# Decoder trunk on one core: another order of loads, sums and transposes in the opening

## The chip, the cores and the metric

The kernel runs on one core of one Trainium2 chip. The metric is the device time of one execution in microseconds (us), lower is better. One profiled execution supplies every duration that is read from a trace.

## What is computed

The reference is a trunk of two decoder layers on one sequence of 256 positions and width 2048, in float32. The first layer mixes tokens by forgetting attention with 16 heads, the second by sliding-window attention with sinks. Each is followed by a gated feed-forward layer of width 5632 with a causal convolution of width 3. Every sub-layer is shifted, scaled and gated by vectors that come from one conditioning vector `c`.

```python
c_act = jax.nn.silu(c)
for i in range(DEPTH):                                   # DEPTH = 2
    mod = c_act @ ada_w[i] + ada_b[i]                    # (1, 2048) @ (2048, 12288)
    sh1, sc1, g1, sh2, sc2, g2 = jnp.split(mod[:, None, :], 6, axis=-1)
    h = x * (1.0 + sc1) + sh1
    y = fox_attention(h, ...) if i % 2 == 0 else swa_attention(h, ...)
    x = layer_norm(ALPHA * x + (1.0 + g1) * y, ln_mix_g[i], ln_mix_b[i])
    h = x * (1.0 + sc2) + sh2
    y = conv_ffn(h, ffn_w_up[i], ffn_conv_w[i], ffn_conv_b[i], ffn_w_down[i])
    x = layer_norm(ALPHA * x + (1.0 + g2) * y, ln_ffn_g[i], ln_ffn_b[i])
```

The change lies in the very first of these lines: shift and scale of layer 0 (`sh1`, `sc1`), the modulated input `h`, and the first products `h @ w_in` of the forgetting attention. What is computed stays the same.

## The kernel before, in words

Almost every product is made in three parts: the float32 weight tile `w` (256 rows by 512 columns, 512 KB) is loaded by the SyncE queue, ScalarE casts it to its high part `wh` (line 276), VectorE subtracts to get the low part `wl` (line 287), and TensorE multiplies high by high, high by low and low by high. The modulated input stands as a high and a low part too (`hHL`). One weight tile with its matmuls is called a product below. Ten tile buffers of 512 KB (the pool `wp`) hold all weights in flight, whatever their use; four `wh` and four `wl` buffers stand behind them.

Attention can start only when `h` is there, and `h` needs shift and scale, which are themselves a product of a vector with 2048 rows of `ada_w`. The function `opening` does this in eight steps. Step `cb` deals with one chunk of 256 columns of shift and 256 of scale: sixteen loads `wo` of 128 rows by 512 columns (256 KB each, two to a tile buffer, line 532), each multiplied by its element of `cact` and added to an accumulator `oacc` of 128 by 512. That is done by `sums`: GpSimd writes the accumulator by the first multiply (line 542), VectorE adds the other fifteen in order (line 547; one of them, row block 10 of step 0, is summed by TensorE instead, line 539). At the end of a step comes what is called a turn below: TensorE sums the accumulator over the partitions with four matmuls of one column against `ones` (tile `cps`, line 572; as float32 each is recorded as two passes), transposes two blocks of `x` (`mod_turn`, line 469, tile `sm`), VectorE adds the bias (`cv`, line 578) and `mod_pair` makes the high and low parts of `h` for these 256 columns (lines 478 to 482 in step 0, 484 to 486 and 85 to 86 later).

Beside the sums, steps 1 to 8 run products of the forgetting attention that need only chunks which are already turned. The table `plan` (line 860) names two items for each of the steps 1 to 7 and one for step 8; an item is three products (q, k, v), so six products fall on a step. Where an item's block of outputs is left for another, ScalarE copies its partial sums out of PSUM (line 886, tiles `part` and `spare`). `warm` (line 494) issues matmuls whose result nobody reads, to keep TensorE busy before real work. `x` is loaded 512 columns at a time, ahead of the even steps (line 567). `rotary` (lines 170 to 205) prepares tables for the second layer; its first two VectorE instructions (lines 176 and 178) wait for two small loads.

The program fixes the order of an engine's instructions where `pin` is used; elsewhere a list scheduler decides it when the program is built. The engines then run their own queues in order. After the opening the kernel goes on with products of the same kind to its end.

Of the kernel before, what the change touches and what calls it, by code (L numbers as in the profile page):

```python
# [17 lines left out]
P = 128  # L18
# [23 lines left out]
def hybrid_trunk(ctx: ExitStack, tc: tile.TileContext, a: dict, out: bass.AP):  # L42
# [127 lines left out]
    def rotary():  # L170
# [5 lines left out]
        nc.vector.tensor_scalar_mul(nsink, sink, -1.0)  # L176
        posf = cst.tile([NT, P], F32, name="posf")
        nc.vector.tensor_copy(posf, posr)
# [341 lines left out]
    def opening(plan, proj, also):  # L520
# [5 lines left out]

        def sums(cb, acc, ps):
            for kq in range(0, KC, QK):
                w = wp.tile([P, QK, 2, CB], F32, tag="w", name="wo")
                for k in range(QK):  # L530
                    kc = kq + k
                    nc.sync.dma_start(w[:, k], a["ada_w"][0, kc * P:(kc + 1) * P, :2 * D]
                                      .rearrange("p (v d) -> p v d", v=2)[:, :, cb * CB:(cb + 1) * CB])
                for k in range(QK):
                    kc = kq + k
                    wk = w[:, k].rearrange("p v f -> p (v f)")
                    if cb == 0 and kc == 10:
                        for c in range(4):
                            pin(mm(ps[:, c:c + 1], wk[:, c * P:(c + 1) * P], cact[:, kc:kc + 1], start=c == 0, skip_group_check=True))
                        warm(6)  # L540
                    elif kc == 0:
                        nc.gpsimd.tensor_scalar_mul(acc, wk, cact[:, kc:kc + 1])  # L542
                    elif cb == 1 and kc == 1:
                        with tc.issue_after(first_cv[0].ins):
                            nc.vector.scalar_tensor_tensor(acc, wk, cact[:, kc:kc + 1], acc, op0=ALU.mult, op1=ALU.add)
                    else:
                        nc.vector.scalar_tensor_tensor(acc, wk, cact[:, kc:kc + 1], acc, op0=ALU.mult, op1=ALU.add)  # L547
                yield

        first_cv = []  # L550
        accs = cst.tile([P, D], F32, tag="acc", name="oacc").rearrange("p (c a) -> p c a", a=2 * CB)
        for cb, items in enumerate(plan):
            k = 2 * cb
            todo = [(*it, part) for it in items for part in range(3)]
            n = len(todo)
            if cb == D // CB:
                for it in todo:
                    proj(*it)
                break
            acc = accs[:, cb % 4]  # L560
            ps = bank("cps")
            also.get(cb, lambda: None)()
            steps = [sums(cb, acc, ps)] * (KC // QK)
            for i, g in enumerate(steps):
                if i == 0 and cb % 2 == 0:
                    c = slice(cb * CB, (cb + 2) * CB)
                    nc.sync.dma_start(x[:, :, c], a["x"][0][:, c].rearrange("(t p) d -> p t d", p=P))
                next(g)
                while todo and n - len(todo) < (i + 1) * n // len(steps):
                    proj(*todo.pop(0))  # L570
            for c in range(4):
                pin(mm(ps[:, c:c + 1], acc[:, c * P:(c + 1) * P], ones[:, 0:1], start=cb > 0 and c == 0, stop=True,
                       skip_group_check=True), cb == 0)
            if cb == 0:
                warm(8)
            tps = mod_turn(k, 2 if cb == 0 else 1)
            for v in range(2):
                first_cv[:] = [nc.vector.scalar_tensor_tensor(cols[0, v][:, k:k + 2], ps[:, 2 * v:2 * v + 2], float(v),
                                                              acol[:, 0, v * KC + k:v * KC + k + 2],
                                                              op0=ALU.add, op1=ALU.add)]  # L580
            mod_pair(cols[0, 1], cols[0, 0], k, tps, cb == 0)
# [569 lines left out]
```

## Time and profile before

| | us |
|---|---|
| median of 3 runs (2270.6 to 2272.76) | 2271.17 |
| the profiled execution | 2271.15 |
| its span, first to last instruction | 2269.4 |
| TensorE busy / weight loads busy | 2202.8 / 1889.6 |
| VectorE busy | 1863.2 |
| ScalarE busy | 1184.0 |
| GpSimd busy | 35.7 |
| first product of the attention starts at | 30.76 |

How to read it: the profiled execution's own time is 1.75 us above its span and 0.02 us below the median, so a microsecond of its span counts as a microsecond of the median. Times in the rows are counted from the span's start. A row of the timeline gives start, duration, engine, line, operation, output and inputs, shape and count; in brackets stands how long the engine had been idle before it, and what ended that wait. Rows of several instructions are merged.

### The profile page before, as it was taken

The numbers are of one execution on the slowest core, as the hardware profiler recorded it, in microseconds if no ns is written. First come the engines' busy times: TensorE is split into PE (matmuls) and PEld (weight loads), VectorE is DVE, ScalarE is ACT, GpSimd is POOL, SyncE is SP. The second block draws the span as 40 slices with busy tenths as digits, with TensorE's granted clock in tenths as the row PEclk, the third lists the DMA queues.
The fourth block names the chain that finished last, engine by engine and source line by source line (L and its number), as shares of the span: only waits on it lengthen the run. The fifth ranks groups of instructions, "written<-read, shape, count | busy, mean of one in ns | idle before, by whom it ended". The sixth has DMA issues, their size and how long they took to land. (4 is left out here: it accounts for less than half of the span.)

```text
span 2269.4 us, 33231 instructions
## 1 busy us (share of the span) xinstructions
PE 2202.8 (97%) x12135; PEld 1889.6 (83%) x12135; DVE 1863.2 (82%) x2692; ACT 1184.0 (52%) x1859; POOL 35.7 (2%) x59
## 2 busy tenths in 40 slices
PE   5899999999999999999999999999999999999997
PEld 5789898788888888888887788888888888888886
DVE  6898998979988978878988989889988655666766
ACT  2435644455555533555534588746555533555642
POOL 1110000000000000000000000000000000000000
PEclk9999999999999999999999999999999999999999
DMA  9999999968977889878887876668887556666553
GB/s 333 346 336 323 346 354 356 323 233 293 327 254 249 300 315 324 284 241 280 283 299 278 271 239 225 232 252 288 285 275 243 185 193 191 190 189 194 187 195 111
DMA packets 287012, 602.67 MB, mean 266 GB/s; under 512 B 21814, under 2 KB 54776, under 8 KB 286336
## 3 DMA queue, kind: packets, MB, share of 16 engines
q1 hardware_dynamic: 285792, 595.86, 77.5%
q0 software_dynamic: 1056, 4.69, 0.6%
q8 instruction: 95, 1.56, 0.3%
q14 instruction: 69, 0.57, 0.1%
HBM read 598.37 MB, written 2.10 MB: 265 GB/s over the span
## 5 line engine op out<-in xcount | busy, mean ns | idle before, releaser
L276 ACT CAST wh<-w 128x1024 fp32r<-128x1024 f32 x728 | 763.5, 1051 | 789.0 <-PE wd L76 284.1
L287 DVE TENSOR_TENSOR wl<-w,wh 128x1024 fp32r<-128x1024 f32 x728 | 887.0, 1221 | 296.2 <-ACT wh L276 281.1
L76 PE MATMUL wd<-hHL,wh 128*128 128x512 f32 x2816 | 717.9, 397 | 1.1 <-DVE hHL L482 1.1
L76 PEld LDWEIGHTS wd<-hHL,wh 128*128 128x128 f32 x2816 | 503.5, 188 | 100.0 <-issue 2.9
L76 PEld LDWEIGHTS wd<-hHL,wl 128*128 128x128 f32 x2816 | 373.2, 188 | 32.8 <-DVE wl L287 1.6
L76 PE MATMUL wd<-hHL,wl 128*128 128x256 f32 x2816 | 379.6, 277 | 1.1 <-DVE wl L287 1.1
L406 DVE SCALAR_TENSOR_TENSOR acc<-wa,cact,acc 128x1024 f32<-128x1024 f32 x300 | 380.4, 1277 | 0.0
L76 PE MATMUL xs<-wh,gT 128*128 128x512 f32 x1408 | 349.7, 390 | 0.0
L76 PEld LDWEIGHTS xs<-wh,gT 128*128 128x128 f32 x1408 | 263.4, 188 | 54.2
L76 PE MATMUL xs<-wl,gT 128*128 128x512 f32 x704 | 189.3, 389 | 0.0
L76 PE MATMUL xs<-wh,hHL 128*128 128x512 f32 x704 | 185.2, 400 | 2.8 <-DVE hHL L86 2.7
L76 PEld LDWEIGHTS xs<-wl,gT 128*128 128x128 f32 x704 | 132.1, 188 | 27.6
L76 PEld LDWEIGHTS xs<-wh,hHL 128*128 128x128 f32 x704 | 129.0, 190 | 29.1 <-DVE hHL L86 3.5
L76 PE MATMUL ws<-hHL,wh 128*128 128x256 f32 x1024 | 134.9, 284 | 7.8 <-ACT wh L276 7.5
L1041 ACT ACTIVATE u<-s,ccol 128x256 f32<-128x256 f32 x176 | 104.6, 599 | 66.7 <-DVE s L1036 49.0
L76 PEld LDWEIGHTS ws<-hHL,wh 128*128 128x128 f32 x1024 | 126.2, 192 | 12.3 <-ACT wh L276 10.6
L76 PE MATMUL xs<-wl,hHL 128*128 128x512 f32 x352 | 98.5, 400 | 1.5 <-DVE wl L287 1.4
L76 PE MATMUL xs<-wh,oT 128*128 128x512 f32 x384 | 98.8, 395 | 0.1
L547 DVE SCALAR_TENSOR_TENSOR oacc<-wo,cact,oacc 128x512 f32<-128x512 f32 x118 | 89.5, 759 | 7.3 <-POOL oacc L542 4.9
L1042 DVE SCALAR_TENSOR_TENSOR u<-s,ccol,u 128x255 f32<-128x255 f32 x176 | 84.0, 479 | 5.6 <-ACT u L1041 5.6
L1044 DVE SCALAR_TENSOR_TENSOR u<-s,ccol,u 128x254 f32<-128x254 f32 x176 | 83.8, 477 | 1.1
L76 PEld LDWEIGHTS xs<-wh,oT 128*128 128x128 f32 x384 | 69.9, 188 | 14.0 <-ACT pT L694 0.6
(223 smaller groups left out, 1641.8 us busy)
## 6 DMA issues: line engine op xcount, KB each, us to landing
w<-in_ffn_w_up_dram SPq DMA_DIRECT2D x352, 512.0 KB, 4.6
wa<-in_ada_w_dram SPq DMA_DIRECT2D x320, 512.0 KB, 5.1
w<-in_ffn_w_down_dram SPq DMA_DIRECT2D x176, 512.0 KB, 4.4
w<-in_fox_w_in_dram SPq DMA_DIRECT2D x96, 512.0 KB, 6.3
wo<-in_ada_w_dram SPq DMA_DIRECT2D x128, 256.0 KB, 6.3
w<-in_swa_w_in_dram SPq DMA_DIRECT2D x40, 512.0 KB, 5.5
w<-in_fox_w_o_dram SPq DMA_DIRECT2D x32, 512.0 KB, 6.0
w<-in_swa_w_o_dram SPq DMA_DIRECT2D x32, 512.0 KB, 5.1
```

Of the source, the lines that this page charges most:

```text
L76: return nc.tensor.matmul(o, lhsT, rhs, start=start, stop=stop, **kw)
L276: pin(nc.scalar.copy(h, w), False)
L287: pin(nc.vector.tensor_tensor(l, w, f32(h), op=ALU.subtract), go in behind)
L406: pin(nc.vector.scalar_tensor_tensor(ac, wo, cact[:, k:k + 1], ac, op0=ALU.mult, op1=ALU.add), True)
L547: nc.vector.scalar_tensor_tensor(acc, wk, cact[:, kc:kc + 1], acc, op0=ALU.mult, op1=ALU.add)
L1041: nc.scalar.activation(u, s, AF.Identity, bias=cw(CW, f), scale=cw(2, f))
L1042: nc.vector.scalar_tensor_tensor(u[:, 1:], s[:, :S - 1], cw(1, f), u[:, 1:], op0=ALU.mult, op1=ALU.add)
L1044: nc.vector.scalar_tensor_tensor(u[:, 2:], s[:, :S - 2], cw(0, f), u[:, 2:], op0=ALU.mult, op1=ALU.add)
```

## The change

- Step 0 does without GpSimd: VectorE makes the first multiply itself, and TensorE sums row blocks 6 and 10 (before: only 10). VectorE so has 14 instructions there, as before.
- `x` is no longer loaded first. Its first 256 columns come after 14 of the 16 loads of step 0, the next 256 columns at the start of step 1; later loads stay.
- Steps 1 to 7 have two accumulators each, for even and odd row blocks. ScalarE starts both (row blocks 0 and 1), VectorE adds the other fourteen, and the two are summed by eight one-column matmuls in place of four.
- The turn of chunk 0 transposes `x` before the one-column matmuls, and the second `warm` shrinks from 8 to 6 and the first from 6 to 5. The turn of a later chunk is issued in the next step, after its second or third pair of loads (`due`), and its `cv` instructions are pinned.
- The two early instructions of `rotary` are pinned, so that the scheduler no longer moves them ahead.

```diff
-        nc.vector.tensor_scalar_mul(nsink, sink, -1.0)
+        pin(nc.vector.tensor_scalar_mul(nsink, sink, -1.0))
...
-        nc.vector.tensor_copy(posf, posr)
+        pin(nc.vector.tensor_copy(posf, posr))
...
+        def load_x(c0, c1):
+            nc.sync.dma_start(x[:, :, c0:c1], a["x"][0][:, c0:c1].rearrange("(t p) d -> p t d", p=P))
+
         def sums(cb, acc, ps):
+            nq = 1 if cb == 0 else 2
             for kq in range(0, KC, QK):
+                if cb == 0 and kq == KC - QK:
+                    load_x(0, CB)
...
-                    if cb == 0 and kc == 10:
+                    ac = acc[:, kc % nq]
+                    if cb == 0 and kc in (6, 10):
                         for c in range(4):
-                            pin(mm(ps[:, c:c + 1], wk[:, c * P:(c + 1) * P], cact[:, kc:kc + 1], start=c == 0, skip_group_check=True))
-                        warm(6)
-                    elif kc == 0:
-                        nc.gpsimd.tensor_scalar_mul(acc, wk, cact[:, kc:kc + 1])
-                    elif cb == 1 and kc == 1:
-                        with tc.issue_after(first_cv[0].ins):
-                            nc.vector.scalar_tensor_tensor(acc, wk, cact[:, kc:kc + 1], acc, op0=ALU.mult, op1=ALU.add)
+                            pin(mm(ps[:, c:c + 1], wk[:, c * P:(c + 1) * P], cact[:, kc:kc + 1],
+                                   start=kc == 6 and c == 0, skip_group_check=True))
+                        if kc == 10:
+                            warm(5)
+                    elif kc >= nq:
+                        nc.vector.scalar_tensor_tensor(ac, wk, cact[:, kc:kc + 1], ac, op0=ALU.mult, op1=ALU.add)
+                    elif cb == 0:
+                        nc.vector.tensor_scalar_mul(ac, wk, cact[:, kc:kc + 1])
                     else:
-                        nc.vector.scalar_tensor_tensor(acc, wk, cact[:, kc:kc + 1], acc, op0=ALU.mult, op1=ALU.add)
+                        nc.scalar.mul(ac, wk, cact[:, kc:kc + 1])
...
+        def chunk(cb, acc, ps):
+            k, first = 2 * cb, cb == 0
+            if first:
+                tps = mod_turn(k, 2)
+            nq = 1 if first else 2
+            for c in range(4):
+                for q in range(nq):
+                    pin(mm(ps[:, c:c + 1], acc[:, q, c * P:(c + 1) * P], ones[:, 0:1],
+                           start=not first and c == q == 0, stop=q == nq - 1, skip_group_check=True), first)
+            if first:
+                warm(6)
+            else:
+                tps = mod_turn(k)
+            for v in range(2):
+                pin(nc.vector.scalar_tensor_tensor(cols[0, v][:, k:k + 2], ps[:, 2 * v:2 * v + 2], float(v),
...
+            mod_pair(cols[0, 1], cols[0, 0], k, tps, first)
...
-            acc = accs[:, cb % 4]
-            ps = bank("cps")
+            acc = accs[:, cb % 2]
+            ps = bank("cps") if cb == 0 else None
...
-                if i == 0 and cb % 2 == 0:
-                    c = slice(cb * CB, (cb + 2) * CB)
-                    nc.sync.dma_start(x[:, :, c], a["x"][0][:, c].rearrange("(t p) d -> p t d", p=P))
+                if i == 0 and cb and cb % 2 == 0:
+                    load_x(cb * CB, (cb + 2) * CB)
+                if i == 0 and cb == 1:
+                    load_x(CB, 2 * CB)
                 next(g)
+                if due and i == (1 if cb in (2, 4) else 2):
+                    due()
+                    due = None
...
-            for c in range(4):
-                pin(mm(ps[:, c:c + 1], acc[:, c * P:(c + 1) * P], ones[:, 0:1], start=cb > 0 and c == 0, stop=True,
-                       skip_group_check=True), cb == 0)
             if cb == 0:
-                warm(8)
-            tps = mod_turn(k, 2 if cb == 0 else 1)
...
+                chunk(cb, acc, ps)
+            else:
+                due = lambda cb=cb, acc=acc: chunk(cb, acc, bank("cps"))
```

What the scheduler makes of it is seen in the order of the instructions. First TensorE, from the sums of step 0 to the first products (`ws` and `xs` are outputs of products), before the change:

```order
L76 MATMUL cps<-cact,wo 128x1 x4
L76 MATMUL warm<-ones 128x512 x6
L76 MATMUL cps<-ones,oacc 128x1 x4
L76 MATMUL warm<-ones 128x512 x8
L469 MATMUL sm<-ident,x 128x128 x4
L76 MATMUL ws<-hHL,wh 128x256 x18
```

The same place with the change:

```order
L76 MATMUL cps<-cact,wo 128x1 x8
L76 MATMUL warm<-ones 128x512 x5
L469 MATMUL sm<-ident,x 128x128 x4
L76 MATMUL cps<-ones,oacc 128x1 x4
L76 MATMUL warm<-ones 128x512 x6
L76 MATMUL ws<-hHL,wh 128x256 x16
```

The transposes of `x` have moved ahead of the one-column matmuls, and `warm` stands directly before the first product.

Second TensorE at the turn of chunk 2, from the tenth product on, before the change:

```order
L76 MATMUL ws<-hHL,wh 128x256 x16
L76 MATMUL ws<-hHL,wl 128x256 x8
L76 MATMUL cps<-ones,oacc 128x1 x4
L469 MATMUL sm<-ident,x 128x128 x4
L76 MATMUL ws<-hHL,wh 128x256 x16
```

The same chunk's turn with the change, from the eleventh product on:

```order
L76 MATMUL ws<-hHL,wh 128x256 x16
L76 MATMUL ws<-hHL,wl 128x256 x8
L76 MATMUL cps<-ones,oacc 128x1 x8
L469 MATMUL sm<-ident,x 128x128 x4
L76 MATMUL xs<-wh,hHL 128x512 x8
```

The turn stands one product later and has eight one-column matmuls.

Third ScalarE around the copies of the partial sums of the third item (products seven to nine), before the change:

```order
L276 CAST wh<-w 128x1024 x2
L886 COPY part<-ws 128x512 x2
L276 CAST wh<-w 128x1024
L886 COPY part<-ws 128x512 x2
L886 COPY part<-xs 128x512 x2
L276 CAST wh<-w 128x1024 x3
```

With the change (line 886 has become 911):

```order
L276 CAST wh<-w 128x1024
L911 COPY part<-ws 128x512 x2
L276 CAST wh<-w 128x1024
L911 COPY part<-ws 128x512 x2
L276 CAST wh<-w 128x1024
L911 COPY part<-xs 128x512 x2
L276 CAST wh<-w 128x1024 x2
```

One cast has moved ahead of the copy of `xs`; before, three casts stood behind it.

19 lines of the change are left out of this document (8 added, 11 removed).

## The prediction

> **What bounds the kernel now.** First the stages, by the view of busy time in windows: the start until the first product, the rest of the opening, what follows at once, and the long remainder.
>
> ```profile
> 0.00:31.00 31.00, 11.74 (x38) 9.19 (x38) 15.48 (x26) 3.38 (x5) 7.15 (x22) 1.00 0.97 335
> 31.00:190.00 159.00, 142.96 (x990) 131.06 (x990) 140.18 (x184) 70.38 (x88) 15.11 (x11) 0.97 1.00 344
> 190.00:450.00 260.00, 250.58 (x1620) 224.40 (x1618) 243.30 (x344) 136.10 (x242) 5.30 (x11) 0.99 0.94 337
> 450.00:2250.00 1800.00, 1791.57 (x9468) 1520.29 (x9467) 1449.01 (x2115) 973.83 (x1526) 6.24 (x13) 1.00 0.74 249
> ```
>
> Behind the length stand the busy times of TensorE, weight loads, VectorE, ScalarE and GpSimd, then TensorE's granted clock, the DMA share and GB/s. From 31 us on TensorE is the engine that is always near full: it idles 9.4 of 260 us and 8.4 of 1800 us after the opening. So what the opening ends earlier, the kernel ends earlier; later stages give nothing and take nothing. In the opening TensorE idles 16.0 of 159 us, and DMA (share 1.00) and VectorE (88%) stand close behind it. Before 31 us it does nothing that counts.
>
> Second the start, by the timelines of TensorE, VectorE, ScalarE, GpSimd and the SyncE queue.
>
> ```profile
> 16.37 2.91 PE L76 MATMUL warm<-ones 128*128 128x512 f32 x6
> 23.26 1.86 PE L76 MATMUL cps<-ones,oacc 128*128 128x1 f32 x8 [3.98 <-DVE oacc L547]
> 24.99 3.76 PE L76 MATMUL warm<-ones 128*128 128x512 f32 x8
> 28.55 0.97 PE L469 MATMUL sm<-ident,x 128*128 128x128 f32 x4
> 30.76 0.50 PE L76 MATMUL ws<-hHL,wh 128*128 128x256 f32 x2 [1.25 <-ACT wh L276]
> ```
> ```profile
> 8.64 3.17 DVE L547 SCALAR_TENSOR_TENSOR oacc<-wo,cact,oacc 128x512 f32<-128x512 f32 x4 [4.95 <-POOL oacc L542]
> 14.60 0.18 DVE L176 TENSOR_SCALAR nsink<-sink 128x32 f32<-128x32 f32 x1 [2.79 <-DMA sink<-in_swa_sinks_dram]
> 15.07 8.13 DVE L547 SCALAR_TENSOR_TENSOR oacc<-wo,cact,oacc 128x512 f32<-128x512 f32 x10
> 25.16 0.23 DVE L578 SCALAR_TENSOR_TENSOR cv<-cps,acol 128x2 f32<-128x2 f32 x2 [1.96 <-PE cps L76]
> ```
> ```profile
> 29.21 0.56 ACT L478 ACTIVATE hHL<-sm,cv 128x256 fp32r<-128x256 f32 x1 [26.61 <-PE sm L469]
> 29.68 1.03 ACT L276 CAST wh<-w 128x1024 fp32r<-128x1024 f32 x1
> ```
> ```profile
> 7.03 1.57 POOL L542 TENSOR_SCALAR oacc<-wo,cact 128x512 f32<-128x512 f32 x1 [4.08 <-DMA wo<-in_ada_w_dram]
> ```
> ```profile
> 2.13 13.47 SPq L532 DMA_DIRECT2D wo<-in_ada_w_dram  x20
> 15.97 0.37 SPq L273 DMA_DIRECT2D w<-in_fox_w_in_dram  x1
> ```
>
> The sums of step 0 end at 23.20 (15.07 and 8.13), held by GpSimd's first multiply (VectorE starts at 8.64) and by 2.79 us for a load that nobody needs yet. Then one thing follows another: one-column matmuls, `warm`, transposes, modulation (29.21), cast (29.68), first product (30.76). `cv` was there at 25.39, but `h` had to wait until `warm` and the transposes were through.
>
> Third the waits of TensorE in the opening, and the groups of its turn.
>
> ```profile
> PE ws L76 <- ACT wh L276: 7.5, 6, 1.6
> PE cps L76 <- DVE oacc L547: 5.1, 3, 1.9
> PE ws L76 <- DVE wl L287: 4.4, 4, 1.7
> ```
> ```profile
> L76 PE MATMUL cps<-ones,oacc 128*128 128x1 f32 x56 | 7.1, 248 | 5.1 <-DVE oacc L547 5.1
> L469 PE MATMUL sm<-ident,x 128*128 128x128 f32 x28 | 4.4, 281 | 0.0
> ```
>
> The columns of the waits are the sum, how often, and the longest; of the groups busy time, mean ns and idle time. The three make 17.0 us, a little over the 16.0 from the windows, since a wait may reach over a window's edge or lie under another's tail; I work with the waits.
>
> **The change part by part.**
>
> *Start.* The loads are issued at 13.47 / 20 = 0.67 us a tile of 256 KB, so 512 KB of `x` in front cost two of these. Without them the first `wo` is there at about 7.03 - 1.35 = 5.7. Its multiply runs on VectorE instead of GpSimd's 1.57 us. From 5.7 on, thirteen adds at 8.13 / 10 = 0.81 us and one multiply of at most that take until 17.0. The last `wo`, 16 tiles after the first since 256 columns of `x` stand between (16 x 0.67 = 10.7), comes at 16.4; add a microsecond for the two small loads that then still share the queues, so the sums end at 17 to 18. Now only the one-column matmuls (1.86) and `cv` (0.23) lie between the sums and the modulation, which could start near 20: transposes and 5 `warm` are done meanwhile, and 6 `warm` run after the one-column matmuls, up to about 22.5. So the product's weights become what is last. Which load takes which place in the queue: before, `x` (two tiles' worth) and 20 `wo` precede the first `w`; with the change 20 `wo` and two halves of `x` do. That is the same place, so `w` is issued at 15.97 as before. The DMA view for that one issue gives its time to landing:
>
> ```profile
> w<-in_fox_w_in_dram SPq DMA_DIRECT2D x1, 512.0 KB, 6.0
> ```
>
> So it lands at 22.0, its cast takes 1.03, and the first product stands at 23.05 instead of 30.76: 7.7 us earlier. The sums have 2 us of room in that. If all of it were eaten, each further microsecond of theirs would cost one.
>
> *Waits for the accumulator (5.1 us, three times).* At the end of a step TensorE comes to the turn, and VectorE has not summed the last `wo`. Issued a step later, the turn finds sums that are long done. Only for the first such turn the order puts it right behind the fourth product, as before; I leave one wait of 5.1 / 3 = 1.7. Gain 3.4. What supports it: VectorE has 14 adds a step instead of 15, and neighbours now go to different accumulators:
>
> ```profile
> 38.97 3.11 DVE L547 SCALAR_TENSOR_TENSOR oacc<-wo,cact,oacc 128x512 f32<-128x512 f32 x4
> 231.34 2.47 DVE L406 SCALAR_TENSOR_TENSOR acc<-wa,cact,acc 128x1024 f32<-128x1024 f32 x2
> 30.46 0.74 DVE L547 SCALAR_TENSOR_TENSOR oacc<-wo,cact,oacc 128x512 f32<-128x512 f32 x1
> ```
>
> Four adds to one accumulator take 3.11, more than 4 x 0.74 = 2.96; two on different halves overlap (they are twice as wide). So VectorE has at least 0.74 us less to do a step. I count it at nothing in the sum: it only keeps VectorE from being the next bound.
>
> *Waits for a cast (7.5 us, six times).* Some come from ScalarE's order: its copy of `xs` waits for TensorE's end, the casts stand behind it, TensorE then waits for them.
>
> ```profile
> 64.12 1.07 ACT L886 COPY part<-xs 128x512 f32<-128x512 f32 x2 [1.44 <-PE xs L76]
> 65.08 2.95 ACT L276 CAST wh<-w 128x1024 fp32r<-128x1024 f32 x3
> 66.19 2.12 PE L76 MATMUL ws<-hHL,wh 128*128 128x256 f32 x16 [1.64 <-ACT wh L276]
> ```
>
> This happens at three items. At two of them the new order has one cast ahead of that copy (shown above for the third item), which takes away 2 x 1.64 = 3.3. The first item keeps its order and its wait. The rest, and the 4.4 for `wl`, I leave.
>
> *ScalarE's multiplies.* Fourteen pieces of some 0.53 us (half of the 1.07 for two copies of the same size), about 1.1 us a step on an engine that is busy 70.38 of 159 us. They wait for loads that come ahead of the casts' own. Value nothing; if each pair delayed a cast that TensorE waits for, 7 x 1.07 = 7.5. A gain of its own it can't be, since it only adds instructions to that queue.
>
> *Doubled one-column matmuls.* Seven turns now have eight instead of four: 7.1 us more on TensorE. Nothing hides that, since it is TensorE's own time: minus 7.1. In step 0, four for row block 6 are added, under the sums.
>
> *Pinned `cv`, later turn.* `cv` stands in VectorE's order and waits for TensorE's turn; adds and `wl` queue behind it, and SyncE for their buffers. VectorE's work left over from a step is what it can lose there, and TensorE has two more products in hand then. Value nothing, from 0 to the 4.4 that `wl` costs today once more.
>
> *Clock.* TensorE's clock falls to half for a stretch after some turns.
>
> ```profile
> 48.00:50.00 2.00, 2.00 (x19) 2.00 (x19) 1.24 (x3) 0.75 (x2) 0.00 (x0) 0.94 1.04 386
> 50.00:52.00 2.00, 2.00 (x11) 2.00 (x11) 1.93 (x5) 2.00 (x3) 0.00 (x0) 0.50 1.01 357
> ```
> ```profile
> 48.97 3.11 PE L76 MATMUL ws<-hHL,wh 128*128 128x256 f32 x16
> 51.87 1.70 PE L76 MATMUL ws<-hHL,wl 128*128 128x256 f32 x8
> 72.06 2.07 PE L76 MATMUL ws<-hHL,wh 128*128 128x256 f32 x16
> 73.97 1.07 PE L76 MATMUL ws<-hHL,wl 128*128 128x256 f32 x8
> 113.68 2.96 PE L76 MATMUL ws<-hHL,wh 128*128 128x256 f32 x16
> ```
>
> The same product takes 3.11 + 1.70 after one turn and 2.07 + 1.07 after the next: 1.7 us lost; the row at 113.68 shows a second such turn. The halved stretch followed a wait of 1.6 us and a turn. The Trainium skill (TensorE: Matmul & The Clock Gate, "HAM oscillation — how this bites in real kernels") puts the limit at an idle gap of about 3.4 us; this trace shows a fall after a wait of half that, so here the turn itself seems to count as idleness. By the page's rule turns without waits cost no clock; today's two halved stretches would go, and the sum below would be larger by 3.4. By the trace, waits go and turns get longer: I take both to cancel.
>
> *The sum:* 7.7 + 3.4 + 3.3 - 7.1 = 7.3 us. Against the profiled execution's 2271.15 that is 2263.8, and as it stands at the median of the runs (2271.17), 2263.8 for the median too. A measurement can tell about 0.2%, 4.5 us, from no change.
>
> **The rivals.**
>
> *More is gained.* If no clock is lost after turns any more (2 x 1.7) and half of the waits for `wl` goes as well (2.2), 12.9 are gained: 2258.3. For it: two of the three waits before a turn go, and VectorE has less to do. Against: `wl` also waits for weights that are late.
>
> *The loads pace the opening.* DMA share is 1.00 between 31 and 190 us, and no byte is saved. If it alone sets the pace, an earlier first product only waits more for later weights, and what stays is a microsecond: 2270.2. Against it speaks the SyncE queue's own view of its waits:
>
> ```profile
> SPq L532 <- DVE wl L287: 17.7, 15, 2.4
> SPq L532 <- DVE oacc L547: 12.7, 16, 4.5
> SPq L273 <- DVE wl L287: 12.1, 14, 2.1
> ```
>
> In 42.5 us it waited for VectorE to free a buffer, so the queue was not always the pace itself; earlier sums free buffers earlier.
>
> *Slower: the turns halve the clock.* A turn becomes 2.0 + 0.6 us long in which the array hardly works (2 x 7.1 / 7 and 4.4 / 7), with no wait needed. If every one of the seven costs two halved stretches of 1.7, that is 23.8 against 3.4 after two turns today, 20.4 more: 7.3 - 20.4 = -13.1, so 2284.3. It decides from eight further stretches on (8 x 1.7 = 13.6 eats the gain and the 4.5). Against: at the turn before 72.06 a wait and a turn cost nothing.
>
> **How the numbers follow.** The forecast has 0.60, more gained 0.13, loads pace 0.17, clock 0.10. Of the forecast 0.56 lies beyond 4.5 us of gain and 0.04 within; more gained is faster throughout; of the pacing case 0.03 is faster, 0.12 the same, 0.02 slower; of the clock case 0.03 is the same and 0.07 slower. Faster 0.72, same 0.19, slower 0.09. The range goes from 2257.5, the case of more gained, to 2270.5, the paced one, which also takes in the 7.5 for ScalarE; the clock case and the tails are left out.
>
> **What would show it.** Right: the first `ws` product near 23, behind a cast that waited for the load of `w`; no wait of `cps` for `oacc` but one; 112 passes in the group of `cps`; TensorE's idle time between the first product and the last of the opening near 10 us instead of 16. The forecast is wrong if the first product is early and TensorE's waits for `wh` have grown by as much (loads), or if the granted clock shows a half after most turns.

## The result and the profile after

The changed kernel takes 2255.66 us in the median of four runs (2254.79 to 2256.26), beside 2271.24 for the kernel before. The ratio is 0.993, with a 95% interval of 0.9913 to 0.9947. It is 15.6 us faster, twice what was forecast (7.4). The profiled execution's span went from 2269.4 to 2254.5 us.

The stages first, in the windows that the prediction showed of the kernel before (TensorE, weight loads, VectorE, ScalarE, GpSimd, granted clock, DMA share, GB/s).

```profile
0.00:31.00 31.00, 17.97 (x88) 15.57 (x88) 19.32 (x32) 8.18 (x11) 3.86 (x20) 1.00 0.93 311
31.00:190.00 159.00, 152.08 (x1132) 142.88 (x1131) 136.58 (x183) 85.83 (x107) 3.70 (x8) 0.99 1.04 374
190.00:450.00 260.00, 250.40 (x1570) 222.29 (x1570) 242.68 (x345) 130.77 (x234) 4.10 (x9) 0.99 0.94 340
450.00:2250.00 1800.00, 1782.77 (x9413) 1512.20 (x9411) 1452.40 (x2129) 968.92 (x1522) 8.24 (x15) 1.00 0.74 247
```

Everything happens in the opening: DMA moves 374 GB/s there instead of 344, and TensorE is busy 152.08 of 159 us instead of 142.96. (In the last row the changed kernel's end moves into the window: its last product is done near 2241, that of the kernel before near 2256.)

Fixed windows hold different work in the two kernels. So here is the same piece of the program, from the first product to the first matmul of the forget gate (`lg`), of the kernel before and then of the changed one.

```profile
30.76:192.10 161.34, 145.29 (x1009) 133.40 (x1010) 142.52 (x187) 72.47 (x91) 15.11 (x11) 0.97 1.00 343
```
```profile
25.17:177.30 152.13, 145.21 (x1064) 136.01 (x1065) 133.14 (x180) 80.67 (x102) 2.52 (x5) 0.99 1.06 383
```

This is the whole balance. The first product is 30.76 - 25.17 = 5.6 us earlier. TensorE's busy time in between is the same. Its idle time falls from 161.34 - 145.29 = 16.05 to 152.13 - 145.21 = 6.92 us, which is 9.1. Together that makes 14.7, and `lg` indeed begins at 177.30 instead of 192.10. VectorE has 142.52 - 133.14 = 9.4 us less to do in that piece, and the DMA runs at 383 GB/s instead of 343.

The start, by the timelines of the SyncE queue, GpSimd, VectorE, ScalarE and TensorE of the changed kernel (start, length, what, and in brackets the idle time before it and what ended that):

```profile
1.65 10.51 SPq L538 DMA_DIRECT2D wo<-in_ada_w_dram  x14
...
18.06 0.37 SPq L273 DMA_DIRECT2D w<-in_fox_w_in_dram  x1
```
```profile
2.91 0.72 POOL L172 DMA_DIRECT2D sink<-in_swa_sinks_dram  x1
...
3.92 0.53 POOL L174 DMA_DIRECT2D posr<-in_positions_dram  x1
```
```profile
5.10 0.75 DVE L551 SCALAR_TENSOR_TENSOR oacc<-wo,cact,oacc 128x512 f32<-128x512 f32 x1
9.81 3.11 DVE L551 SCALAR_TENSOR_TENSOR oacc<-wo,cact,oacc 128x512 f32<-128x512 f32 x4 [3.96 <-DMA wo<-in_ada_w_dram]
...
18.74 1.54 DVE L551 SCALAR_TENSOR_TENSOR oacc<-wo,cact,oacc 128x512 f32<-128x512 f32 x2 [0.41 <-DMA wo<-in_ada_w_dram]
```
```profile
24.07 1.05 ACT L276 CAST wh<-w 128x1024 fp32r<-128x1024 f32 x1 [0.36 <-DMA w<-in_fox_w_in_dram]
```
```profile
20.34 1.87 PE L76 MATMUL cps<-ones,oacc 128*128 128x1 f32 x8
22.07 2.91 PE L76 MATMUL warm<-ones 128*128 128x512 f32 x6
25.17 2.10 PE L76 MATMUL ws<-hHL,wh 128*128 128x256 f32 x13 [0.19 <-ACT wh L276]
```

As the prediction had it, the cast of the first `w` is what comes last, and it waits for that load. It is last by only 0.19 us, though: the sums end at 20.28 (18.74 + 1.54) and not at 17 to 18, so the six `warm` behind them run until 24.98. And `w` is issued at 18.06 instead of 15.97, and VectorE stands idle for 3.96 us behind its second block. GpSimd no longer multiplies, so it does not wait for the first `wo`, and its two small loads go out at 2.91 and 3.92 instead of 8.85 and 9.62, into the first weights. The windows of one microsecond (same columns as above) show what the DMA did then.

```profile
5.00:6.00 1.00, 0.00 (x0) 0.00 (x0) 0.82 (x2) 0.00 (x0) 0.00 (x0) 1.00 0.84 172
6.00:7.00 1.00, 0.00 (x0) 0.00 (x0) 0.00 (x0) 0.00 (x0) 0.00 (x0) 1.00 0.66 176
7.00:8.00 1.00, 0.00 (x0) 0.00 (x0) 0.00 (x0) 0.00 (x0) 0.00 (x0) 1.00 0.75 200
```

In the kernel before these three read 330, 349 and 352 GB/s. Next TensorE's waits in the opening (sum, times, longest), and three of its groups.

```profile
PE ws L76 <- ACT wh L276: 4.7, 3, 2.8
PE ws L76 <- DVE hHL L86: 2.0, 2, 1.0
PE ws L76 <- ACT hHL L85: 0.3, 1, 0.3
```
```profile
L76 PE MATMUL ws<-hHL,wh 128*128 128x256 f32 x496 | 65.2, 283 | 7.1 <-ACT wh L276 4.7 <-DVE hHL L86 2.0 <-ACT hHL L85 0.3
L76 PE MATMUL ws<-hHL,wl 128*128 128x256 f32 x248 | 34.1, 281 | 0.0
...
L76 PE MATMUL cps<-ones,oacc 128*128 128x1 f32 x112 | 13.1, 243 | 0.0
```

No wait of `cps` for `oacc` and none of `ws` for `wl` is left; two waits for `hHL` are new, each a product behind a turn. The same three groups of the kernel before read 66.4, 37.2 and 7.1 us busy. So the doubled column sums are there (56 to 112 passes, 6.0 us more), and the `ws` products took 4.3 us less; in the granted clock three halved stretches of 3.4 us have become one. And the waits of the SyncE queue between 31 and 190:

```profile
SPq L538 <- DMA wo<-in_ada_w_dram: 19.0, 71, 0.9
SPq L273 <- DMA w<-in_fox_w_in_dram: 18.7, 22, 1.0
SPq L538 <- DMA w<-in_fox_w_in_dram: 12.7, 15, 0.9
SPq L400 <- DVE wl L287: 11.1, 6, 5.3
SPq L273 <- DVE wl L287: 7.2, 10, 2.7
...
SPq L538 <- DVE oacc L551: 3.4, 10, 0.8
```

In the kernel before the three longest of these waits were for VectorE (17.7, 12.7, 12.1). Now they are for the DMA itself: the queue is no longer kept from issuing by a buffer that VectorE holds, it waits for earlier loads to make room. The longest wait for VectorE that is left (11.1) belongs to `wa` (L400), behind the opening's own sums.

### The profile page after: what moved, and what is told of

Same layout as the page of the kernel before. It is cut to its first block, busy times and chain, and to the rows that moved or that the text cites. A ratio compares the mean times of both kernels' runs of the same rounds, so it can differ in the third digit from the quotient of the medians.

```text
span 2254.5 us, 33348 instructions
## 1 busy us (share of the span) xinstructions
PE 2203.2 (98%) x12196; PEld 1892.9 (84%) x12196; DVE 1852.2 (82%) x2685; ACT 1193.7 (53%) x1873; POOL 19.9 (1%) x51
## 5 line engine op out<-in xcount | busy, mean ns | idle before, releaser
L551 DVE SCALAR_TENSOR_TENSOR oacc<-wo,cact,oacc 128x512 f32<-128x512 f32 x111 | 79.5, 746 | 15.1 <-DMA wo<-in_ada_w_dram 10.0
```

The costliest lines, as they stand in the source:

```text
L551: nc.vector.scalar_tensor_tensor(ac, wk, cact[:, kc:kc + 1], ac, op0=ALU.mult, op1=ALU.add)
```

## The experiments

The forecast erred by being too small, so the question was which part brought the rest. Theory A: VectorE's part sets the pace, because it gives back the load buffers. Theory B: the place of the turn at the step's end sets it. The column "`lg` at" of the table is the start of the first `lg` matmul in the profile, where the opening is over; what lies behind it takes 2075 to 2078 us in the profiles of all kernels but those with nine buffers (2087 and 2086). Two profiles of the changed kernel lie 2.7 us apart there, so differences below that are not read from this column. Kernels were timed on several chips, on which the kernel before took 2271.2 to 2273.5 us; so the ratio to it is what compares them.

The column "clock" is an estimate, good to about 1 us, from the granted clock that is recorded of each run (to 0.001): (1 - clock) times the span, in the mean of the runs, is the time that TensorE lost at half clock. It counts halved idle time, too: some 5 us are the same everywhere, since the clock is halved over the last ten microseconds of every kernel, where TensorE has nothing left to do.

| kernel | us, median | ratio to before (95%) | `lg` at | clock |
|---|---|---|---|---|
| before | 2271.24 | 1 | 192.1 | 13.6 to 15.3 |
| changed | 2255.66 | 0.9930 (0.9913 to 0.9947) | 177.3 | 10.1 |
| changed, again | 2255.89 | 0.9923 (0.9911 to 0.9936) | 180.0 | 8.6 |
| start alone | 2264.14 | 0.9964 (0.9951 to 0.9977) | 184.8 | 10.9 |
| later turn alone | 2266.66 | 0.9975 (0.9965 to 0.9985) | 187.6 | 13.3 |
| two accumulators alone | 2264.93 | 0.9969 (0.9959 to 0.9979) | 186.0 | 10.1 |
| changed, one accumulator | 2262.62 | 0.9958 (0.9943 to 0.9972) | 183.7 | 12.4 |
| changed, small loads later | 2254.66 | 0.9921 (0.9904 to 0.9937) | 176.4 | 9.6 |
| changed, turn at the end | 2257.97 | 0.9938 (0.9923 to 0.9953) | 182.4 | 9.0 |
| changed, 21 more adds | 2261.14 | 0.9953 (0.9939 to 0.9968) | 186.0 | 11.3 |
| changed, VectorE begins | 2256.82 | 0.9931 (0.9916 to 0.9946) | 178.1 | 10.7 |
| changed, one after the other | 2259.86 | 0.9941 (0.9929 to 0.9954) | 182.2 | 10.8 |
| changed, gate's loads later | 2253.48 | 0.9910 (0.9897 to 0.9924) | 174.9 | 7.9 |
| both later loads | 2251.09 | 0.9902 (0.9887 to 0.9917) | 172.8 | 7.9 |
| both, turn a product earlier | 2249.78 | 0.9904 (0.9889 to 0.9919) | 172.8 | 7.9 |
| before, nine buffers | 2283.35 | 1.0049 (1.0033 to 1.0066) | 195.6 | 21.7 |
| changed, nine buffers | 2263.18 | 0.9960 (0.9944 to 0.9976) | 176.8 | 13.6 |

### The three parts, each alone

*Start alone*, on the kernel before:

```diff
+                if cb == 0 and kq == KC - QK:
+                    load_x(0, CB)
...
-                    if cb == 0 and kc == 10:
+                    if cb == 0 and kc in (6, 10):
...
+                    elif cb == 0:
+                        nc.vector.tensor_scalar_mul(ac, wk, cact[:, kc:kc + 1])
```

> Only the start of the change: step 0 without GpSimd, x behind its weights, transposes ahead of the one-column matmuls, the two small rotary instructions in order. Steps 1 to 7 keep GpSimd's first multiply, one accumulator and the turn at the step's end. All theories: first product near 25.2 us, 5.6 us earlier than before. If VectorE's adds or the turn's place set the pace of the steps, the kernel keeps between 3 us (VectorE's first cv is 2.9 us earlier) and 5.6 us of that: 2265.6 to 2268. If the loads alone set the pace from 31 us on, next to nothing: 2270.

*Later turn alone*, with one accumulator and GpSimd's multiply as before:

```diff
-            for c in range(4):
-                pin(mm(ps[:, c:c + 1], acc[:, c * P:(c + 1) * P], ones[:, 0:1], ...))
...
+                if due and i == (1 if cb in (2, 4) else 2):
+                    due()
+                    due = None
```

> Only the turn a step later: start as before, one accumulator started by GpSimd, four one-column matmuls. Theory A (VectorE's own work a step, 15 adds in one chain, sets the pace): little, 2266 to 2270. Theory B (what set the pace was the turn at the step's end, where TensorE waited 5.1 us for VectorE's sums and VectorE 9.7 us for TensorE's one-column matmuls): most of the 10 us that the change gains after the first product, near 2261.

*Two accumulators alone*, begun by ScalarE (so GpSimd is rid of its multiply there, too), with start and turn as before:

```diff
-                    elif kc == 0:
-                        nc.gpsimd.tensor_scalar_mul(acc, wk, cact[:, kc:kc + 1])
+                    ac = acc[:, kc % nq]
...
+                        nc.scalar.mul(ac, wk, cact[:, kc:kc + 1])
```

> Only the accumulators: ScalarE starts two of them in each of steps 1 to 7, VectorE adds fourteen, eight one-column matmuls at a turn; start and turn's place as before. Theory A: VectorE is rid of 0.74 us and of the gaps between adds to one accumulator, so 1.5 to 1.8 us a step, and most of the 10 us is gained, 2261 to 2264. Theory B: the turn stays where it was, TensorE pays 5.9 us for doubled one-column matmuls and VectorE waits longer for them: 2271 to 2277.

Measured against the kernel before on the same chip (2272.65): 8.5, 6.0 and 7.7 us faster. The start alone is worth about what the prediction gave it (7.7), and more than was expected of it here. That is partly luck: the first product stands at 25.01 there, 5.8 us earlier and not 7.7, and the rest came with a clock that lost less (10.9 us, and 15.1 in the kernel before on that chip). The later turn lies between the two theories, nearer to A. The two accumulators, which by theory B should bring nothing or less, bring as much as the start. Together 8.5 + 6.0 + 7.7 = 22.2, but the whole change gains 15.6 (17.6 in its second timing): each part relieves something that another part relieves too. Waits that end in a halved clock are one such thing: start and accumulators alone each save 4 to 5 us by the column "clock", and so does the whole change.

### The whole change less one part

*One accumulator*, begun by ScalarE:

```diff
-            nq = 1 if cb == 0 else 2
+            nq = 1
...
-            acc = accs[:, cb % 2]
+            acc = accs[:, cb % 4]
```

> The changed kernel with one accumulator in place of two: ScalarE starts it, VectorE adds fifteen in one chain, four one-column matmuls at a turn. Theory A: VectorE's steps are longer by 0.7 to 1.7 us each, 2259 to 2266. Theory B: TensorE is rid of 5.9 us of one-column matmuls and nothing else changes, near 2250.

*Turn at the end of its own step* (the later `cv` are left to the scheduler again, as in the kernel before):

```diff
-            if cb == 0:
-                chunk(cb, acc, ps)
-            else:
-                due = lambda cb=cb, acc=acc: chunk(cb, acc, bank("cps"))
+            chunk(cb, acc, ps)
```

> The changed kernel with the chunk's turn back at the end of its own step (start and two accumulators kept). Theory A (VectorE's time per step sets the pace): the two accumulators keep most of what they bring beside the start, 2258 to 2260, with 8 to 12 us of VectorE waits for cps back. Theory B (the place of the turn sets the pace): the accumulators bring nothing while the turn stands at the end, 2263 to 2265 as with the new start alone.

Without the second accumulator 6 to 8 us of the gain are gone by the ratios (0.9958 against 0.9930 and 0.9923, times 2271). Without the later turn it is 2 to 3. With the turn at the end VectorE waits for it as it did before, in fact longer (before it was 10.5 us over the same window, 25 to 176):

```profile
DVE cv L575 <- PE cps L76: 14.8, 7, 2.4
```

and still the kernel keeps most of the gain. So the turn's place is not what mainly held the kernel, although the later turn alone was worth 6.0: theory B falls as the whole account, and A needs to say what of VectorE it was.

### What of VectorE

*21 more adds* (a block times zero added to its accumulator, which changes no result):

```diff
+                        if cb and kc in (5, 9, 13):
+                            nc.vector.scalar_tensor_tensor(ac, wk, 0.0, ac, op0=ALU.mult, op1=ALU.add)
```

> The changed kernel with three more adds of VectorE in each of steps 1 to 7 (a block times zero is added to its accumulator, so the result is the same): 21 adds of 0.745 us, 15.6 us of VectorE work. Theory A (VectorE sets the pace, so what the change takes off it counts nearly in full): 8 to 14 us slower than the changed kernel, 2264 to 2270. Rival (the loads now set the pace and VectorE has 20 of 155 us free): 0 to 3 us slower, 2256 to 2259.

*VectorE begins the accumulators:*

```diff
-                        nc.scalar.mul(ac, wk, cact[:, kc:kc + 1])
+                        nc.vector.tensor_scalar_mul(ac, wk, cact[:, kc:kc + 1])
```

> The changed kernel, but VectorE instead of ScalarE begins both accumulators of each later step: 14 multiplies of about 0.7 us go back to VectorE, while the adds still take turns on two accumulators. Theory A1 (what counts is VectorE's time, 16 operations a step at 0.70 us against 14): 5 to 8 us slower than the changed kernel, 2261 to 2264. Theory A2 (what counts is that adds alternate, 0.66 us from one to the next instead of 0.78): within 2 us of it, 2254 to 2258, and the 4.3 us that VectorE waits for ScalarE's multiplies are gone.

*One accumulator after the other* instead of in turn:

```diff
-                    ac = acc[:, kc % nq]
+                    ac = acc[:, kc // (KC // nq)]
...
-                    elif kc >= nq:
+                    elif kc % (KC // nq):
```

> The changed kernel with its two accumulators used one after the other (blocks 0 to 7 on the first, 8 to 15 on the second) instead of in turn: the same operations, buffers, ScalarE multiplies and doubled column sums, but each add now follows one on its own accumulator (0.78 us from add to add instead of 0.66). Theory A2 (the alternation itself brings what the two accumulators bring): 4 to 6 us slower than the changed kernel. Theory A3 (VectorE's time a step counts only above what the loads leave it; 14 adds at 0.78 are 10.9 us a step, as with VectorE's own multiplies, which cost nothing): 0 to 2 us slower.

The adds in the profile of the first and the multiplies in that of the second, as groups (busy, mean ns) and as a tile's forms (min/median/max ns):

```profile
L553 DVE SCALAR_TENSOR_TENSOR oacc<-wo,oacc 128x512 f32<-128x512 f32 x21 | 14.5, 689 | 0.5
```
```profile
L555 DVE TENSOR_SCALAR oacc<-wo,cact x12: 478/484/489, 43.7 to 143.6; 128x512 f32<-128x512 f32 x12
```

14.5 us of extra adds cost 5 to 7 by the ratios, between the 8 to 14 of theory A and the 0 to 3 of its rival: VectorE's time counts, but only about 40% of it arrives at the end. Each of these adds also follows one to its own accumulator, so this kernel breaks the alternation as well. The multiplies (0.48 each, not the 0.7 that I had expected) cost nothing that can be told. The 4.3 us that VectorE waits for ScalarE in the changed kernel go at the same time, so the two may offset each other; but it is not VectorE's busy time as such that counts.

The third was timed beside the changed kernel on one chip:

> The changed kernel unaltered, timed beside the three below: 2254 to 2257 us, ratio to the kernel before near 0.993.

It has the same operations as the changed one, and no more of them. It is 4.0 us slower (2259.86 against 2255.89; the two intervals overlap a little, the runs themselves do not). Two adds behind each other, in the changed kernel and then in this one:

```profile
27.21 1.40 DVE L551 SCALAR_TENSOR_TENSOR oacc<-wo,cact,oacc 128x512 f32<-128x512 f32 x2
```
```profile
27.31 1.53 DVE L551 SCALAR_TENSOR_TENSOR oacc<-wo,cact,oacc 128x512 f32<-128x512 f32 x2
```

So it is the alternation that brings at least a good part of what the second accumulator brings, and the reading that it costs nothing as long as the loads leave room (0 to 2 us) falls. What this kernel can't tell apart is the shorter pairs and the place of the second multiply, which here stands in the middle of a step on ScalarE. Nor does the loss arrive as idle time alone. By the column "clock" some 2.3 of the 4.0 us are TensorE at half clock, and the two profiles have two halved stretches in the opening against none. Whether the longer adds bring these stretches about, by way of longer waits, or chance does, is not shown.

### Is it the buffers?

The same cut, nine load buffers instead of ten, in the kernel before and in the changed one.

```diff
-    wp = ctx.enter_context(tc.tile_pool(name="wp", bufs=10))
+    wp = ctx.enter_context(tc.tile_pool(name="wp", bufs=9))
```

> The kernel before with nine buffers for loads instead of ten; nothing else is altered. Theory (what held the kernel before in the opening was how soon VectorE gives back a load's buffer; SyncE's queue waited 48 us for VectorE between 25 and 176): a buffer less is asked for earlier still, that wait grows and the opening ends 4 to 10 us later, 2275 to 2282. Rival (TensorE's own order sets the pace and the loads run far enough ahead): within 2 us of the kernel before at the end of the opening.

> The changed kernel with nine buffers for loads instead of ten. Theory (its loads run at the pace of the DMA, SyncE waits only 12 to 20 us for VectorE): it loses less than the kernel before does from the same cut, 1 to 5 us at the end of the opening. Rival (buffers still hold it as before): as much as the kernel before loses.

First the kernel before with nine, then the changed one with nine: the first `lg` matmuls, and the SyncE queue's waits between 31 and 190.

```profile
L76 PE MATMUL lg<-hHL,fh x32: 276/276/277, 195.6 to 200.8; 128*128 128x256 f32 x32
```
```profile
SPq L273 <- DVE wl L287: 20.2, 19, 2.4
SPq L532 <- DVE oacc L547: 15.6, 23, 2.5
SPq L532 <- DVE wl L287: 12.4, 9, 2.0
```
```profile
L76 PE MATMUL lg<-hHL,fh x32: 276/276/276, 176.8 to 182.0; 128*128 128x256 f32 x32
```
```profile
SPq L538 <- DMA wo<-in_ada_w_dram: 20.7, 71, 1.8
SPq L273 <- DMA w<-in_fox_w_in_dram: 17.3, 20, 1.0
SPq L538 <- DMA w<-in_fox_w_in_dram: 12.0, 15, 0.9
```

The opening of the kernel before ends 3.5 us later with a buffer less, a little under the 4 expected; that of the changed one not at all (176.8, against 177.3 and 180.0). Most of what both lose in the median (12 us, to 2283.35 and so past the range expected, and 7 us) is lost behind the opening, where the same buffers carry other loads; by the column "clock" some 8 and 4 us of it are TensorE at half clock. With one profile each this agrees with the theory that VectorE's hold on the buffers paced the kernel before, and no longer does. It does not prove it: 3.5 us is not far beyond the scatter of 2.7.

### What paces the opening now

*Small loads later* (sink and posr wait until chunk 7's columns are there, by a copy into their tiles):

```diff
+        nc.vector.tensor_copy(sink[:, 0:2], cols[0, 1][:, KC - 2:KC])
         nc.gpsimd.dma_start(sink, a["swa_sinks"][0].partition_broadcast(P))
```

> The changed kernel, but GpSimd's two small loads (sink and posr, issued at 2.91 and 3.92 us in the changed kernel) wait until chunk 7's columns are written, so that nothing but the opening's weights is loaded at the start. Theory: these two loads hold the first weights of x back (wo's third block lands at 9.72 us, 172 GB/s in 5:6), so without them the first w lands near 22.0 instead of 24.05 and the first product begins near 23.1 instead of 25.17; the loads pace the opening from there on, so the gain stays to the end: 2253.6 us. Rival: the slow first microseconds come from the order of the opening's own loads, or an earlier start is waited off before the normalised input is ready: first product within 0.3 us of 25.17, 2255.7.

*The gate's loads later* (the five of `bfc` and `wf`, behind step 7's weights):

```diff
+                also[cb]()
...
-        opening(plan, first_block, {6: forget_load})
+        opening(plan, first_block, {8: forget_load})
```

> The changed kernel, with the five loads of the forget gate (bfc, wf) issued behind step 7's weights instead of at the start of step 6, where the DMA falls to 166 GB/s in 115:120 and TensorE then waits 2.8 us for wh and runs 3.4 us at half clock. Theory (the loads pace steps 1 to 7 now): 2.5 to 5 us faster than the changed kernel. Rival (the hole in the loads is covered by buffers or comes back later): within 1 us of it.

*Both:*

> Both later loads in one kernel (sink and posr after the opening, bfc and wf behind step 7's weights). Theory (the loads pace the opening): the two gains add, 3.5 to 7 us faster than the changed kernel, 2249 to 2252. Rival: one of them only moves a wait, 1 to 3 us faster.

With the small loads out of the way, in the timelines of SyncE and TensorE and in the windows:

```profile
16.30 0.37 SPq L275 DMA_DIRECT2D w<-in_fox_w_in_dram  x1
```
```profile
23.41 2.60 PE L76 MATMUL ws<-hHL,wh 128*128 128x256 f32 x16 [2.25 <-ACT wh L278]
```
```profile
6.00:7.00 1.00, 0.00 (x0) 0.00 (x0) 0.29 (x2) 0.00 (x0) 0.00 (x0) 1.00 0.96 299
```

`w` is issued at 16.30 and the first product stands at 23.41, 1.8 us earlier; 299 GB/s instead of 176 in that microsecond. This repeats: the three kernels with the small loads later begin their first product at 22.5 to 23.4, the nine with the new start, ten buffers and these loads early at 25.0 to 26.2. In the median it is 1.0 us, which by itself can't be told from nothing. The gate's loads, in the changed kernel and in the one that has them later:

```profile
115.00:120.00 5.00, 5.00 (x47) 5.00 (x46) 4.31 (x5) 1.55 (x2) 0.00 (x0) 1.00 0.84 166
```
```profile
115.00:120.00 5.00, 5.00 (x45) 4.83 (x43) 4.76 (x6) 1.98 (x2) 0.00 (x0) 1.00 1.07 388
```

The hole in the DMA goes, and 2.4 us of time on the same chip (just under what was expected). Both together give 2251.09, 4.8 us less than the changed kernel beside it and 22.4 less than the kernel before. With the gate's loads out of the way the small loads are worth 2.4 us (2253.48 against 2251.09, and no run of the one reaches those of the other). So what the loads gain in the opening now arrives at the end, and they pace it, though not alone: 21 more adds of VectorE still cost 5 to 7.

The Trainium skill (DMA: Bandwidth & Descriptors, "Why small descriptors are slow (HBM only)") gives every packet a fixed overhead, 27% for a descriptor of 256 bytes. For the gate's loads the direction agrees: from 114 to 121 us, 2247 of 3142 packets are under 512 bytes, with these loads later 121 of 2055. It does not explain the start. In the kernel before, the same two small loads went out at 8.85 and 9.62, among the same `wo`, and there the DMA kept its rate (the lowest of the next microseconds was 317, in 13 to 14):

```profile
9.00:10.00 1.00, 0.00 (x0) 0.00 (x0) 0.96 (x2) 0.00 (x0) 0.99 (x2) 1.00 1.10 381
10.00:11.00 1.00, 0.00 (x0) 0.00 (x0) 0.96 (x2) 0.00 (x0) 0.15 (x1) 1.00 1.08 381
```

Why they cost the DMA half its rate in the first microseconds and little afterwards, no run here shows.

*Turn a product earlier*, with both later loads:

```diff
-                if due and i == (1 if cb in (2, 4) else 2):
+                if due and i == (0 if cb in (2, 4) else 1):
```

> The kernel with both later loads (sink, posr; bfc, wf), and each chunk's turn issued one product earlier in the next step, since TensorE still waits twice 1.0 us for hHL (VectorE's second shift and scale of a chunk) right behind a turn. Theory: these two waits go, 1 to 2 us faster than without this. Rival: the turn then comes before VectorE has finished the sums of the step, and waits for oacc come back: 0 to 4 us slower.

The two waits for `hHL` go, but the waits for `wh` rise from 2.2 to 4.9 us, and the ratios are 0.9904 and 0.9902. Nothing is gained: the `lg` matmuls begin at 172.8 with and without. Neither side had expected that; no wait for `oacc` came back, so the rival's reason did not come either.

## Why the prediction was right and wrong

The direction and the place were right: all of the gain lies in the opening, and nothing is given back behind it. The size was off by 8 us. Put beside each other on TensorE, from the start to the first `lg`:

| | forecast | profile |
|---|---|---|
| first product earlier by | 7.7 | 5.6 |
| less idle time | 3.4 + 3.3 = 6.7 | 9.1 |
| more busy time | 7.1 | 0 (-0.1) |
| sum | 7.3 | 14.8 |

So the start fell short by 2.1, the waits gave 2.4 more, and the 7.1 that were charged to TensorE's own time did not come. The steps, one by one:

- *Start, 7.7.* The mechanism was right; the first product came 5.6 us earlier, not 7.7. The step that failed is "That is the same place, so `w` is issued at 15.97 as before". The place in SyncE's queue is the same, but the rate was not: GpSimd's queue, now free of its wait, sent its small loads 6 us earlier. The "microsecond for the two small loads" was put on the sums only, and too small. Shown by the kernel with these loads later. The sums themselves ended at 20.28, so their "2 us of room" were nearly used up. At the end of the opening the new start alone is worth 7.3 (192.1 - 184.8).
- *Waits, 3.4 + 3.3 of 17.* Idle time fell by 9.1, not 6.7. The steps "I leave one wait of 1.7" and "the rest, and the 4.4 for `wl`, I leave" failed: no wait for the accumulator and none for `wl` is left, while two waits for `hHL` (2.0) are new. The waits for a cast fell by 2.8 in this profile, near the forecast 3.3.
- *VectorE's relief, counted "at nothing in the sum".* This step failed too: without the alternation alone 4.0 us of the gain are gone, without the second accumulator 6 to 8. I had seen that VectorE would have at least 0.74 us a step less to do, and that SyncE waited 42.5 us for it to free buffers, but used the second only against a rival and never joined the two. VectorE's busy time fell by 9.4 us over the same piece, SyncE's long waits for it went, the DMA rose from 343 to 383 GB/s, and casts and `wl` found their weights earlier. The kernels with more adds and with adds that do not alternate show that VectorE's time arrives at the end in part; the one in which it makes the multiplies shows that not all of it does. The nine buffers agree on the way it takes. In TensorE's balance it can stand in two places, as fewer waits and as fewer halved stretches behind waits. How much of the 2.4 and of the clock goes back to it is argued from the profile, not shown.
- *Clock, "I take both to cancel".* In TensorE's balance this is the largest term that was mis-sized: they do not cancel, and 3.4 more, the other value that the prediction names, came out in the profile. The case against, that turns without waits halve the clock, didn't come: the turn at 61.72, 1.84 + 0.63 us long, is followed by a product at full speed.

```profile
61.72 1.84 PE L76 MATMUL cps<-ones,oacc 128*128 128x1 f32 x16
63.42 0.63 PE L469 MATMUL sm<-ident,x 128*128 128x128 f32 x4
63.81 2.07 PE L76 MATMUL xs<-wh,hHL 128*128 128x512 f32 x8
```

  Three halved stretches in the opening before became one. That is 2 x 1.7 = 3.4 us of TensorE, and it accounts for most of why TensorE's busy time stayed the same though the column sums grew by 6.0. It is not only this one profile: by the column "clock" the changed kernel loses 8.6 to 10.1 us and the kernel before 13.6 to 15.3. Counted from each matmul's start to the next one's, so without the overlap of their ends, the column sums cost 5.6 more and the `ws` products take 5.6 less. The clock is 3.4 of that; the other 2.2 I can't assign.
- *Doubled column sums, -7.1.* 6.0, since sixteen passes in a row take 1.84 us and eight 1.02, less than double. Near enough.
- *ScalarE's multiplies and the pinned `cv`, nothing.* Right: VectorE no longer waits for `cps` at all in the opening, and the multiplies cost nothing that can be told on VectorE instead.

Of the rivals, *more is gained* named two of the sources (the clock and the waits for `wl`) and stayed 2.7 us short in the median (12.9 against 15.6 us of gain). *The loads pace the opening* was half right: they do now, but since they also run faster, this did not eat the early start. *Slower, by the clock*, did not come.

## What to carry to other kernels

When a load queue waits for an engine to free its buffers, that engine's time can be worth something at the end even if no arithmetic engine waits for it in the list of waits; put a price on it before writing "nothing". Where waits go, clock can come back as well: here it was a term as large as that of a whole part of the change. A queue that a change sets free does what it has to do earlier, and what it sends (here two small loads) meets whatever is now under way, which can cost more there than it did before. Single parts that each gain well need not add up: after the first, another resource sets the pace, and it is worth looking at what holds that one back.

## What the runs showed of the hardware

Adds of VectorE to one accumulator follow each other every 0.78 us, adds that alternate between two every 0.66 to 0.67 (the pairs above: 1.53 and 1.40 us). It holds for the whole opening: of the adds that directly follow one another, 53 of 55 start 0.78 or 0.79 us apart in the kernel before, and 41 of 42 start 0.66 to 0.68 apart in the changed one. The Trainium skill (VectorE: DVE Perf Modes, "The DRAIN you can't avoid") says that the next operation does not start until the pipeline is empty, and adds that one which is not held starts earlier; for 8 copies it measured the same time with a semaphore behind each and with one at the end. The pairs here differ by 0.13 us in nothing but the accumulator they go to, so an add that needs the one before it does cost more.

The clock's fall after a wait depends on more than the wait. The changed kernel was profiled twice, and in both TensorE waited for the same cast behind the gate's loads. Its product behind a wait of 2.81 us ran at half clock in the first profile, and behind a longer one of 3.04 us at full clock in the second:

```profile
127.37 3.08 PE L76 MATMUL ws<-hHL,wh 128*128 128x256 f32 x16 [2.81 <-ACT wh L276]
```
```profile
128.70 2.10 PE L76 MATMUL ws<-hHL,wh 128*128 128x256 f32 x16 [3.04 <-ACT wh L276]
```

The Trainium skill (TensorE: Matmul & The Clock Gate, "What's actually happening") says that activity is judged in windows of 3.4 us that run freely and do not begin with the kernel. These two rows agree with that, and the clock that the traces record shows the windows themselves. In the kernel before, the halved stretches begin at 32.70, 49.77, 114.62, 234.09 and 418.41 us and last 3.41 each, and from each start to the next it is a whole multiple of 3.41 us (5, 19, 35 and 54 times). Laid over the waits, the same step puts 2.5 of the 2.81 us into one window (124.85 to 128.26, where the halved stretch begins), and splits the 3.04 us into 1.5 and 1.5. So in these two rows it is the place of the wait that decides, and not its length alone. How much of a window has to be idle, they do not show.
